# A hybrid decoder trunk on one core: the down projection's B22 loaded twice, and the sums for X3 and X4 moved by one product

## The chip, the cores and the metric

The kernel runs on one core of a Trainium2 chip. The metric is the device time of one execution in microseconds; lower is better. Times of several runs are told as their median. The profile is of one further execution. Engines are called PE (TensorE), PEld (its weight loads), DVE (VectorE), ACT (ScalarE), POOL (GpSimd) and SP (SyncE).

## What is computed

Two layers of a decoder trunk on x of 512 tokens by 1024, all in float32. Each layer is a half-step FFN, a mixer (layer 0 a convolution and a gated unit, layer 1 a multi-scale pool), cross-attention to 256 memory tokens, and a second half-step FFN. So there are four FFNs, and they are where the change lies:

```python
def swiglu_ffn(h, w_gu, w_down):
    gu = h @ w_gu
    gate, up = jnp.split(gu, 2, axis=-1)
    return (jax.nn.silu(gate) * up) @ w_down

f = swiglu_ffn(rms_norm(h, ffn1_pre_g[i]), ffn1_w_gu[i], ffn1_w_down[i])
h = h + 0.5 * rms_norm(f, ffn1_post_g[i])
```

The hidden width is 2816, that is 22 blocks of 128.

## The kernel before

*Precision.* Each float32 operand is split (`split`, L73 to 75) into a rounded part hi, an ACT copy (L74), and the rest lo, a DVE subtraction (L75). A product is three matmuls (`mm3`, L77 to 81: hi by hi, hi by lo, lo by hi). Weights are loaded raw by DMA and split on the chip into `whi` and `wlo`, which have four buffers each (`N_W`); the raw buffers are seven (`N_R`, tag "raw"), each of 512 KB over 128 partitions. Every load of weights in the kernel takes its buffer from these seven.

*An FFN* (`ffn`, L556) goes through the hidden blocks in three parts (`FF_PARTS`): blocks 0 to 7, 8 to 15 and 16 to 21. In each part the gate and up columns are computed in groups of two blocks (`seven`, L292; the very first group by `fm_quad`), and then the part's share of the down projection. For the first two parts the down projection is `seven_tm` (L336): a 2 by 2 block product with seven multiplications where eight are usual. There are four FFNs with two such parts each, eight *down parts* in all. The first of an FFN (`fresh`) writes its results into `f` by ACT copies (L387), the second adds to or subtracts from `f` on DVE (L389, L391).

*A down part.* Weights are the four blocks B11, B12, B21, B22 of 512 rows by 512 columns, each in two raw buffers (two halves of 256 rows, index `kk`). `load` issues plain loads from SP's queue (L347), `put` a second load onto the same buffers that adds to what lies there, from POOL's queue (L352). T1 = B12 + B11 so comes from two loads, T3 = B12 + B22 likewise, and later B21 is added onto T1, which by then is B12 + B11 + B22 (the add of L404, on DVE). X1 to X4 are sums of the activation's quarters: `e` (L394, L400, L417) for X1, X2 and X4, and `r11 -= r21` (L414) for X3; `operand` splits them into buffers of the tag "big". The seven products in order are

| product | bank | weights | operand | result goes to |
|---|---|---|---|---|
| 1 | A | B11 | A11 | f(0,0) |
| 2 | C | T1 | X1 | f(1,1) |
| 3 | A | T1 + B22 | X2 | f(0,1) |
| 4 | B | B21 | A12 | f(0,0) |
| 5 | A | T3 | X3 | f(1,1) |
| 6 | C | B22 | X4 | f(0,1) |
| 7 | A | T1 + B22 + B21 | A22 | f(1,0) |

Each product is 24 matmuls of 512 columns, the first 12 with the first half of the weights (`kk` = 0), and `take` moves or adds its bank's result, one half (`s_`) after the other.

*Order and buffers.* The kernel is written on a layer that gives out tiles' buffers, sets all semaphore waits and puts each engine's instructions in an order of its own: the text sets the precedence, and an instruction may go ahead of earlier ones of its engine that still wait for inputs. Each engine then runs its queue strictly in that order. A raw buffer comes free when the last instruction that reads it has run. In the text before the change, B22's two buffers are loaded once (L358) and read twice: by the adds of L404, and by the split for product 6.

Of the kernel before, what the change touches and what calls it, by code (L numbers as in the profile page):

```python
# [35 lines left out]
def trunk_kernel(tc, x, mem, ffn1_pre_g, ffn1_w_gu, ffn1_w_down, ffn1_post_g,  # L36
# [8 lines left out]
    with ExitStack() as es:  # L45
# [18 lines left out]
        def big(dt=F32R, shape=(P, 4, SEQ)):  # L64
            return sp.tile(list(shape), dt, name="big", tag="big")

        def qt(shape, dt=F32):
            return qp.tile(list(shape), dt, name="q4", tag="q4")
# [4 lines left out]
        def split(hi, lo, src):  # L73
            nc.scalar.copy(out=hi, in_=src)  # L74
            nc.vector.tensor_tensor(out=lo, in0=src, in1=hi.bitcast(F32), op=ALU.subtract)  # L75

        def mm3(ps, lhs, rhs, start, stop, grouped=True):  # L77
            skip = not grouped
            nc.tensor.matmul(out=ps, lhsT=lhs[0], rhs=rhs[0], start=start, stop=skip, skip_group_check=skip)  # L79
            nc.tensor.matmul(out=ps, lhsT=lhs[0], rhs=rhs[1], start=False, stop=skip, skip_group_check=skip)  # L80
            nc.tensor.matmul(out=ps, lhsT=lhs[1], rhs=rhs[0], start=False, stop=stop or skip, skip_group_check=skip)  # L81
# [26 lines left out]
        def ops4():  # L108
            return big(F32R, (P, 2, 4, HALF))
# [124 lines left out]
        def raw_tile(shape):  # L234
            return wp.tile(list(shape), F32, name="raw", tag="raw", bufs=N_R)
# [9 lines left out]
        def parts(raw, shape):  # L245
            hi = wp.tile(list(shape), F32R, name="whi", tag="whi")
            lo = wp.tile(list(shape), F32R, name="wlo", tag="wlo")
            split(hi, lo, raw)
            return hi, lo
# [20 lines left out]
        def psa():  # L270
            return pa.tile([P, 512], F32, name="psa", tag="a")
# [64 lines left out]
        def seven_tm(w, k0, r, a11, f, fresh):  # L336


            def rows(kh, kk, ch):
                u = k0 + 4 * kh + 2 * kk  # L340
                return w[u * P:(u + 2) * P, ch * 512:(ch + 1) * 512].rearrange("(k p) n -> p k n", p=P)

            def load(kh, ch):
                raws = []
                for kk in range(2):
                    raws.append(raw_tile([P, 2, 512]))
                    nc.sync.dma_start(out=raws[kk], in_=rows(kh, kk, ch))  # L347
                return raws

            def put(raws, kh, ch):  # L350
                for kk in range(2):
                    nc.gpsimd.dma_start(out=raws[kk], in_=rows(kh, kk, ch), accum_op=ALU.add)  # L352

            sub, add = ALU.subtract, ALU.add
            t1 = load(0, 1)
            put(t1, 0, 0)
            b11 = load(0, 0)
            b22 = load(1, 1)  # L358
            b21 = load(1, 0)
            r11, r12, r21, r22 = r[0][:, :, :HALF], r[1][:, :, :HALF], r[0][:, :, HALF:], r[1][:, :, HALF:]  # L360

            def operand(src):
                o = ops4()
                split(o[:, 0], o[:, 1], src)
                return o

            banks = {}

            def product(n, raws, ops):
                start = n not in banks  # L370
                if start:
                    banks[n] = [psa(), psa()]
                for kk in range(2):
                    wh = parts(raws[kk], (P, 2, 512))
                    for s_ in range(2):
                        for i in range(2):
                            k = 2 * kk + i
                            cs = slice(s_ * P, (s_ + 1) * P)
                            mm3(banks[n][s_], (ops[:, 0, k, cs], ops[:, 1, k, cs]), (wh[0][:, i], wh[1][:, i]),
                                start and k == 0, k == 3, False)  # L380
                return banks[n]

            def take(th, ch, ps, how):
                for s_ in range(2):
                    dst = f[th][:, s_, ch * 512:(ch + 1) * 512]
                    if how is None:
                        nc.scalar.copy(out=dst, in_=ps[s_])  # L387
                    elif how == "from":
                        nc.vector.tensor_tensor(out=dst, in0=ps[s_], in1=dst, op=sub)  # L389
                    else:  # L390
                        nc.vector.tensor_tensor(out=dst, in0=dst, in1=ps[s_], op=how)  # L391

            e = qt([P, 4, HALF])
            nc.vector.tensor_tensor(out=e, in0=r21, in1=r22, op=sub)  # L394
            x1 = operand(e)
            p1 = product("A", b11, a11)
            if fresh:
                f.append(big(F32, (P, 2, D)))
            take(0, 0, p1, None if fresh else add)
            nc.vector.tensor_tensor(out=e, in0=e, in1=r11, op=sub)  # L400
            x2 = operand(e)
            q5 = product("C", t1, x1)
            for kk in range(2):
                nc.vector.tensor_tensor(out=t1[kk], in0=t1[kk], in1=b22[kk], op=add)  # L404
            if fresh:
                f.append(big(F32, (P, 2, D)))
            take(1, 1, q5, None if fresh else add)
            a12 = operand(r12)
            u2 = product("A", t1, x2)
            t3 = load(0, 1)  # L410
            put(t3, 1, 1)
            put(t1, 1, 0)
            take(0, 1, u2, None if fresh else "from")
            nc.vector.tensor_tensor(out=r11, in0=r11, in1=r21, op=sub)  # L414
            x3 = operand(r11)
            take(0, 0, product("B", b21, a12), add)
            nc.vector.tensor_tensor(out=e, in0=e, in1=r12, op=add)  # L417
            x4 = operand(e)
            take(1, 1, product("A", t3, x3), sub)
            a22 = operand(r22)  # L420
            take(0, 1, product("C", b22, x4), "from")
            take(1, 0, product("A", t1, a22), None if fresh else add)
# [133 lines left out]
        def ffn(pre, w_gu, w_down, post_g, nxt):  # L556
            f = []
            for j0, j1 in FF_PARTS:
# [33 lines left out]
                if ending:  # L592
                    nx = nxt()
                    last_weights(w_down, j0, n, wk, False)
                    tm_last(hid, wk, n, post_g, nx, f)
                else:
                    seven_tm(w_down, j0, r, a11, f, not f)
# [442 lines left out]
```

## Time and profile before

| | us |
|---|---|
| median of 3 runs | 2033.12 |
| the runs | 2029.88, 2033.5, 2033.12 |
| the profiled execution | 2035.78 |
| its span, first to last instruction | 2034.1 |
| PE busy | 1962.7 |
| DVE busy | 1488.5 |
| ACT busy | 1037.4 |
| POOL busy | 234.0 |

A busy time is the sum over an engine's instructions, overlaps counted once. "Granted clock" is the share of the full 2.4 GHz that PE was given; at 0.5 it runs at 1.2 GHz. Times in a timeline are us from the start of the span. In a timeline a row is: start, duration, engine, line, operation, written tile and read tiles, shapes, count; in square brackets stands how long the engine had been idle and what ended that. The down parts' first L404 lies at 103.2, 227.6, 833.4, 957.8, 1183.3, 1308.2, 1763.7 and 1888.3 us; "the first part" below is the one at 103, "the second part" that at 227.

### The profile page before, as it was taken

How to read it: one execution, taken by the hardware profiler on the slowest of the kernel's cores; microseconds unless marked ns; L12 is line 12 of the kernel's file. 1: busy time of each engine (PE TensorE's matmuls, PEld its weight loads, DVE VectorE, ACT ScalarE, POOL GpSimd, SP SyncE). 2: the span in 40 equal slices, each digit the busy share in tenths (PEclk: the TensorE clock that was granted, in tenths of full speed). 3: DMA queues.
4: the chain of work that ended last, by engine and by line, in shares of the span. 5: the costliest groups of instructions: out<-in, count | busy, mean ns of one | idle time of the engine just before them, and what ended most of it. 6: DMA issues, size and time to landing. Idle time of an engine off the chain costs nothing. (4 is left out here: it accounts for less than half of the span.)

```text
span 2034.1 us, 31756 instructions
## 1 busy us (share of the span) xinstructions
PE 1962.7 (96%) x12841; PEld 1788.2 (88%) x12841; DVE 1488.5 (73%) x1831; ACT 1037.4 (51%) x1477; POOL 234.0 (12%) x229
## 2 busy tenths in 40 slices
PE   7999999998999999999999999999999999999998
PEld 7979889888878879899898979989878879989797
DVE  6776877799956558777886877787666648776875
ACT  6555445543555355555454555445535545545452
POOL 1111110122011011110101111110000001111100
PEclk9999999999999999999999999999999999999999
DMA  6877685323642145787873668696152225787771
GB/s 198 217 166 198 161 212 155 110 89 124 225 148 94 52 114 139 172 202 181 191 214 73 169 156 204 169 215 197 53 186 73 83 52 145 184 200 198 172 189 44
DMA packets 245929, 311.51 MB, mean 153 GB/s; under 512 B 9500, under 2 KB 189300, under 8 KB 244758
## 3 DMA queue, kind: packets, MB, share of 16 engines
q1 hardware_dynamic: 189158, 233.93, 35.9%
q0 software_dynamic: 56448, 75.51, 21.9%
q8 instruction: 100, 1.64, 0.3%
q14 instruction: 47, 0.39, 0.1%
q10 hardware_dynamic: 176, 0.05, 0.0%
HBM read 303.15 MB, written 6.29 MB: 152 GB/s over the span
## 5 line engine op out<-in xcount | busy, mean ns | idle before, releaser
L79 PE MATMUL psa<-big,whi 128*128 128x256 f32 (+1 forms) x3056 | 885.2, 291 | 6.2 <-ACT big L74 4.5
L81 PE MATMUL psa<-big,wlo 128*128 128x256 f32 (+1 forms) x3056 | 885.4, 290 | 5.6 <-DVE wlo L75 5.6
L80 PE MATMUL psa<-big,whi 128*128 128x256 f32 (+1 forms) x3056 | 887.1, 291 | 0.8 <-DVE big L75 0.8
L74 ACT CAST whi<-raw 128x1024 fp32r<-128x1024 f32 x522 | 544.3, 1049 | 622.8 <-PE psa L80 275.4
L75 DVE TENSOR_TENSOR wlo<-raw,whi 128x1024 fp32r<-128x1024 f32 x522 | 635.6, 1225 | 283.1 <-ACT whi L74 280.6
L79 PEld LDWEIGHTS psa<-big,whi 128*128 128x128 f32 x3056 | 587.6, 193 | 16.7 <-ACT big L74 8.3
L81 PEld LDWEIGHTS psa<-big,wlo 128*128 128x128 f32 x3056 | 588.0, 193 | 13.6 <-DVE wlo L75 6.7
L80 PEld LDWEIGHTS psa<-big,whi 128*128 128x128 f32 x3056 | 588.7, 193 | 9.1 <-DVE big L75 1.8
L79 PE MATMUL psa<-whi,big 128*128 128x512 f32 x864 | 341.5, 397 | 19.2 <-ACT whi L74 11.5
L80 PE MATMUL psa<-wlo,big 128*128 128x512 f32 x864 | 340.4, 394 | 6.1 <-DVE wlo L75 6.1
L81 PE MATMUL psa<-whi,big 128*128 128x512 f32 x864 | 339.3, 395 | 0.5
L79 PEld LDWEIGHTS psa<-whi,big 128*128 128x128 f32 x864 | 162.9, 189 | 60.7 <-ACT whi L74 16.6
L80 PEld LDWEIGHTS psa<-wlo,big 128*128 128x128 f32 x864 | 164.0, 190 | 42.7 <-DVE wlo L75 9.7
L81 PEld LDWEIGHTS psa<-whi,big 128*128 128x128 f32 x864 | 163.8, 190 | 39.7 <-DVE big L75 5.8
L302 POOL DMA_DIRECT2D raw<-in_ffn_w_gu_dram x40 | 51.6, 1289 | 611.9 <-DMA raw<-in_ffn_w_gu_dram 419.2
L158 POOL TENSOR_TENSOR r<-m,nhalf 128x1 f32<-128x1 f32 x74 | 49.0, 662 | 461.0 <-DVE m L532 182.3
L352 POOL DMA_DIRECT2D raw<-in_ffn_w_down_dram x48 | 57.3, 1193 | 332.7 <-DMA raw<-in_ffn_w_down_dram 229.5
L729 DVE SCALAR_TENSOR_TENSOR big<-big,par 128x511 f32<-128x511 f32 (+29 forms) x120 | 85.7, 767 | 0.0
L79 PE MATMUL psa<-big 128*128 128x512 f32 (+1 forms) x224 | 80.9, 363 | 0.8 <-ACT big L74 0.8
L297 POOL DMA_DIRECT2D raw<-in_ffn_w_gu_dram x40 | 53.0, 1326 | 244.7 <-DMA raw<-in_ffn_w_gu_dram 223.4
L80 PE MATMUL psa<-big 128*128 128x512 f32 (+1 forms) x224 | 80.7, 360 | 0.0
L81 PE MATMUL psa<-big 128*128 128x512 f32 (+1 forms) x224 | 80.2, 359 | 0.0
(150 smaller groups left out, 1658.2 us busy)
## 6 DMA issues: line engine op xcount, KB each, us to landing
raw<-in_ffn_w_gu_dram SPq DMA_DIRECT2D x216, 512.0 KB, 4.8
raw<-in_ffn_w_down_dram SPq DMA_DIRECT2D x104, 512.0 KB, 4.0
raw<-in_ffn_w_gu_dram POOLq DMA_DIRECT2D x80, 512.0 KB, 7.8
raw<-in_ffn_w_down_dram POOLq DMA_DIRECT2D x48, 512.0 KB, 6.1
raw<-in_xa_w_kv_dram SPq DMA_DIRECT2D x32, 512.0 KB, 3.5
raw<-in_ev_w_in_dram SPq DMA_DIRECT2D x16, 512.0 KB, 4.3
raw<-in_xa_w_q_dram SPq DMA_DIRECT2D x16, 512.0 KB, 3.7
raw<-in_xa_w_o_dram SPq DMA_DIRECT2D x16, 512.0 KB, 3.9
```

Of the source, the lines that this page charges most:

```text
L74: nc.scalar.copy(out=hi, in_=src)
L75: nc.vector.tensor_tensor(out=lo, in0=src, in1=hi.bitcast(F32), op=ALU.subtract)
L79: nc.tensor.matmul(out=ps, lhsT=lhs[0], rhs=rhs[0], start=start, stop=skip, skip_group_check=skip)
L80: nc.tensor.matmul(out=ps, lhsT=lhs[0], rhs=rhs[1], start=False, stop=skip, skip_group_check=skip)
L81: nc.tensor.matmul(out=ps, lhsT=lhs[1], rhs=rhs[0], start=False, stop=stop or skip, skip_group_check=skip)
L158: nc.gpsimd.tensor_tensor(out=r, in0=m, in1=nhalf.broadcast_to([P, n]), op=ALU.pow)
L297: nc.gpsimd.dma_start(out=t1, in_=fm_rows(w, 0, ca), accum_op=ALU.add)
L302: nc.gpsimd.dma_start(out=t3, in_=fm_rows(w, 1, cb), accum_op=ALU.add)
L352: nc.gpsimd.dma_start(out=raws[kk], in_=rows(kh, kk, ch), accum_op=ALU.add)
L729: nc.vector.scalar_tensor_tensor(out=acc[:, c, s_:], in0=z[:, c, :SEQ - s_], scalar=par[:, c, CONV - 1 - s_:CONV - s_], in1=acc[:, c, s_:] ...
```

## The change

B22 is loaded a second time, after T3's loads and the second load onto T1; product 6 reads this second load, and the first load is read by the adds of L404 alone. The raw buffers of the first load can then be given to a load that is asked for later, and the next one in the text is T3's. The sum for X3 (L414) and its split now stand in the text behind product 4 and its takes, and the sum for X4 (L417) and its split behind product 5 and its takes; in the text before, each stood ahead of that product. The products, their order and the takes are the same.

```diff
             t3 = load(0, 1)
             put(t3, 1, 1)
             put(t1, 1, 0)
+            b22 = load(1, 1)
             take(0, 1, u2, None if fresh else "from")
+            take(0, 0, product("B", b21, a12), add)
             nc.vector.tensor_tensor(out=r11, in0=r11, in1=r21, op=sub)
             x3 = operand(r11)
-            take(0, 0, product("B", b21, a12), add)
+            take(1, 1, product("A", t3, x3), sub)
             nc.vector.tensor_tensor(out=e, in0=e, in1=r12, op=add)
             x4 = operand(e)
-            take(1, 1, product("A", t3, x3), sub)
             a22 = operand(r22)
             take(0, 1, product("C", b22, x4), "from")
             take(1, 0, product("A", t1, a22), None if fresh else add)
```

## Rows read from the trace of the kernel before

**Rows 1.** The page's first part: busy time, share of span, instructions.
```profile
PE 1962.7 (96%) x12841; PEld 1788.2 (88%) x12841; DVE 1488.5 (73%) x1831; ACT 1037.4 (51%) x1477; POOL 234.0 (12%) x229
```

**Rows 2.** Windows, PE alone: length, busy (matmuls), granted clock, DMA share, GB/s.
```profile
127.70:142.70 15.00, 11.75 (x49) 1.00 0.74 177
252.10:267.10 15.00, 13.37 (x51) 0.89 0.97 236
858.00:873.00 15.00, 11.67 (x50) 1.00 0.72 172
982.30:997.30 15.00, 13.30 (x50) 0.89 0.96 234
1207.80:1222.80 15.00, 12.72 (x47) 0.89 0.69 153
1332.70:1347.70 15.00, 13.36 (x58) 1.00 1.02 255
1788.20:1803.20 15.00, 12.97 (x48) 0.89 0.71 168
1912.80:1927.80 15.00, 13.22 (x57) 1.00 1.00 254
1524.00:1539.00 15.00, 15.00 (x68) 1.00 0.30 95
```

**Rows 3.** Timeline of ACT: T3's hi (first part), X3's hi (second part).
```profile
130.87 1.04 ACT L74 CAST whi<-raw 128x1024 fp32r<-128x1024 f32 x1 [6.43 <-DMA raw<-in_ffn_w_down_dram]
...
247.56 1.05 ACT L74 CAST big<-big 128x1024 fp32r<-128x1024 f32 x1 [1.71 <-PE psa L81]
```

**Rows 4.** Timeline of DVE in the first part.
```profile
104.84 1.23 DVE L404 TENSOR_TENSOR raw<-raw 128x1024 f32<-128x1024 f32 x1
...
131.94 1.23 DVE L75 TENSOR_TENSOR wlo<-raw,whi 128x1024 fp32r<-128x1024 f32 x1 [6.25 <-ACT whi L74]
```

**Rows 5.** Waits of SP's queue, first and second part: total us, times, longest.
```profile
SPq L347 <- DVE wlo L75: 18.7, 2, 16.3
...
SPq L347 <- DVE wlo L75: 22.4, 2, 20.0
```

**Rows 6.** Timeline of POOL in the first part.
```profile
111.63 1.20 POOL L352 DMA_DIRECT2D raw<-in_ffn_w_down_dram  x1 [3.62 <-DVE wlo L75]
...
122.73 1.20 POOL L352 DMA_DIRECT2D raw<-in_ffn_w_down_dram  x1 [6.31 <-DMA raw<-in_ffn_w_down_dram]
```

**Rows 7.** Timeline of DVE in the second part.
```profile
229.16 1.23 DVE L404 TENSOR_TENSOR raw<-raw 128x1024 f32<-128x1024 f32 x1
...
244.04 1.22 DVE L414 TENSOR_TENSOR big<-big 128x1024 f32<-128x1024 f32 x1
...
249.78 1.22 DVE L417 TENSOR_TENSOR q<-q,big 128x1024 f32<-128x1024 f32 x1
...
252.95 0.69 DVE L391 TENSOR_TENSOR big<-big,psa 128x512 f32<-128x512 f32 x1 [0.22 <-PE psa L81]
```

**Rows 8.** All 80 plain loads of L347: time from issue to landing.
```profile
DMA to landing us min/median/max: 3.2/3.9/5.6
```

**Rows 9.** All 48 accumulating loads of L352: time from issue to landing.
```profile
DMA to landing us min/median/max: 5.5/6.1/9.6
```

**Rows 10.** DMA queues from 100 to 150 us: packets, MB, share of 16 engines.
```profile
q1 hardware_dynamic: 4489, 5.20, 33.0%
```

**Rows 11.** Windows, second part: PE, PEld, DVE, ACT, POOL busy, clock, DMA share, GB/s.
```profile
228.00:248.00 20.00, 19.16 (x88) 15.10 (x88) 19.77 (x20) 10.10 (x11) 3.58 (x3) 1.00 0.53 100
248.00:268.00 20.00, 18.37 (x73) 14.39 (x72) 16.82 (x19) 9.06 (x10) 3.42 (x3) 0.91 0.91 238
```

**Rows 12.** The same view, in the gate/up group after the first part.
```profile
148.00:168.00 20.00, 20.00 (x166) 19.88 (x165) 13.24 (x14) 9.97 (x13) 3.14 (x3) 1.00 0.99 222
```

**Rows 13.** The one L352 issued between 238.0 and 239.5 us: time to landing.
```profile
DMA to landing us min/median/max: 5.7/5.7/5.7
```

## The prediction

> **What bounds the kernel now.** I read the page's busy times first. TensorE (PE) is busy 1962.7 of 2034.1 us, DVE 73%, ACT 51% [rows 1]: a PE kernel, so an edit off PE pays only where PE stands still or runs slowly. Busy time hides the second kind (a matmul at half clock counts as busy), so the next view counts matmuls in equal windows. In a stretch without a stall, 15 us hold 68 matmuls of 512 columns. In the eight down parts the 15 us that cover products A (T3, X3) and C (B22, X4) hold 49, 51, 50, 50, 47, 58, 48 and 57 [rows 2]: 410 where 544 would fit, 134 missing. At 15/68 us each, 134 are 29.6 us, 1.5% of the span. 17.2 us of it (78 matmuls) is in the first part of each FFN, whose takes are ACT copies (here "fresh"), 12.4 us (56) in the second. Some of it is clock: in four windows the granted clock is 0.89, so 11% of their 15 us is lost to the lower level (1.2 GHz), after PE had waited in them; in the other four it stays at 1.00 [rows 2].
>
> Who is waited for: in the first part ACT idles 6.43 us for a w_down DMA and starts that buffer's hi copy at 130.87 [rows 3]; DVE, idle for 6.25 us, does its lo at 131.94 [rows 4]; only then can PE go on. The buffer is T3's second half. SP had waited 16.3 us (20.0 us in the second part) before it could issue the plain load, held by a DVE weight split [rows 5]: all seven raw buffers were in use (T1 2, B22 2, B21 2, T3's first half 1), and the next to come free was B21's, split for product B. POOL issued its accumulating load only when the plain one had landed, at 122.73 [rows 6], and that landed 8 us later, at ACT's 130.87.
>
> **The change, part by part.** *T3 early.* B22's first load is no longer read by product C, so its buffers come free at the two adds of L404. The first add ends at 106.07 in the first part [rows 4] and at 230.39 in the second [rows 7]. T3's second half takes that buffer: SP can issue it there, where its waits of 16.3 and 20.0 us [rows 5] ended at about 118.4 and 246.5. A plain load lands in 3.2 to 5.6 us, an accumulating one in 5.5 to 9.6 [rows 8, 9]. With both at their worst and 1 us of POOL, T3 is there at 106.1 + 5.6 + 9.6 + 1 = 122.3, some 8.5 us ahead of today's 130.87, and a fresh part loses only 17.2/4 = 4.3 us. In the second part it is there at 246.6, while PE comes to T3's second half 12 matmuls after 252.9 (where B ends, [rows 7]), at 255.6. So the wait for this DMA goes in all eight parts: up to 29.6 us.
>
> *B22 again.* 2 loads of 512 KB in each of 8 parts, 16 in all. SP's queue moved 5.20 MB in 33.0% of 50 us [rows 10], so 0.524 MB is 1.7 us of all 16 DMA engines, 3.3 us for a part. In the second part the DMA share is 0.53 and then 0.91 over 20 us each [rows 11], 28.8 us of 40; with 3.3 more, in 36.5 us, it is 0.88. Bounds: nothing, or 3.3 x 8 = 27 us if DMA became the bound. I take nothing, because the nearest row is the stretch behind the first part: share 0.99 with PE busy 20.00 of 20 [rows 12]. The first new load gets B22's second old buffer (some 3 us after T3's), the second the B21 buffer that T3's second half has today, at about 246.5. It lands by 252.1; product C starts at 252.9 + 24 x 0.22 = 258.2. Behind it on SP stand the next gate/up loads; today they stand behind T3's load, which waits for the same buffer, so they don't start later. That wait of 20.0 us is the cover; without it each load would cost its issue on SP, under 0.5 us.
>
> *POOL.* T3's second accumulating load moves ahead of T1's two. If POOL waits for T3's plain load (106.1 + 5.6 = 111.7 at worst; T1's first goes at 111.63 today, [rows 6]), T1's come about 1.3 us later, for the last product, over 20 us after. Nothing.
>
> *The sums.* L414 and L417 keep their length (1.22 us each) and move in the text. DVE's queue isn't in text order: L417 stands in the text behind product B's takes and yet ran at 249.78, ahead of the L391 at 252.95 [rows 7]. So an instruction goes in when its inputs are there and nothing ahead of it in the text is ready. Ahead of L414 I expect at most two weight splits and two takes, 1.22 and 0.69 us by the lengths of [rows 7]: 244.04 + 3.8 = 247.9. X3's hi copy starts at 247.56 today [rows 3], so X3 would have its hi at 250.2 and its lo at 251.5; product A (T3, X3) starts at 252.9. No stall, with 1.4 us to spare: bounds 0 and, with L414 behind L391, rival 3. I take 0, by L417's place. In fresh parts DVE has more room (6.25 us idle, [rows 4]).
>
> *What is late next.* DVE. In the second part it is busy 19.77 of 20 and then 16.82 of 20 us [rows 11], 3.41 idle in 40, and the stall to be removed there is 17 matmuls, 3.75 us. It can't all go: DVE would have to work without a gap, while it waits at product ends (0.22 us, [rows 7]). Bounds of what stays: 0 (its last splits belong to the next gate/up group, where DVE is busy 13.24 of 20 us, [rows 12]) to 1.8 us in each such part; I take 0.9, in the middle, 3.6 us for four. For fresh parts 0 to 0.8 each; I take 0.3, 1.2 us, nearer to nothing because of the 6.25 us idle.
>
> **Sum.** 29.6 - 3.6 - 1.2 = 24.8 us. Against the profiled execution's own 2035.78 us: 2011.0. That execution lies 2.7 us above the median of the runs (2033.12; 2029.88 to 2033.5), so for the median 2008.3; I say 2008. Its own range: 2002 (29.6 gone, and runs' spread) to 2014 (the high bounds, 10.4, stay).
>
> **A rule against it.** T3's second accumulating load now goes where DVE is saturated, and it is issued by POOL. The rows speak against a conflict: the one of T1's issued at 238.5, while DVE was busy 19.77 of 20 us [rows 11], landed in 5.7 us [rows 13], near the shortest of all 48, 5.5 [rows 9]. The Trainium skill, "SBUF — State Buffer", § SBUF: two separate sides, warns that a DMA issued from POOL stands still while DVE holds the port that both share, since POOL can't write its descriptors; the page limits that to DVE's 2-port modes. Read broadly it gives rival 2; the trace agrees with the limit.
>
> **Rivals.**
> 1. *DVE takes the stall's place in the second parts.* There nothing is gained, in fresh parts 17.2 - 1.2 = 16.0: 2033.1 - 16.0 = 2017. For it: 19.77 of 20 [rows 11]. Against: over 3 us idle in the 20 that follow. It decides if DVE needs more than the 36.3 us that would be left of the 40. Chance 0.12.
> 2. *T3's early load is starved until DVE pauses* in the second parts, at about 252.7 [rows 7], so lands as late as now: 2017 again. Chance 0.02.
> 3. *The sums stand behind B's takes (slower).* If DVE's queue has L414 after L391, it starts at 252.95 + 0.69 = 253.6, X3's hi is there at 255.9 (1.22 and 1.05 us), its lo at 257.1: product A waits 3.0 us and then some 1.2 more, and the clock falls as in the 0.89 windows, 0.11 x 15 = 1.7 us. 5.9 for the 3.7 removed (29.6/8), +2.2 x 8: 2033 + 18 = 2051. It costs from an L414 start after 250.6 on (252.9 less 1.22 and 1.05). For it: the text now puts it there. Against: L417 [rows 7]. Chance 0.09.
> 4. *The freed buffers don't go to T3* but to another load that asks first; T3's second half waits for B21's as now: 2033. Against: T3's is the oldest load that waits. Chance 0.07.
>
> **How the numbers follow.** Forecast 0.70, with its own time, 2008. The range goes to 2021, over rivals 1 and 2 with the runs' spread of 4 us, and down to 2001 (29.6 gone and a run on the low side of that spread); 3 and 4 are left out, 0.16. A measurement of this kernel tells about 0.2%, 4 us. Faster 0.70 + 0.12 + 0.02 = 0.84, same 0.07, slower 0.09.
>
> **What will show it.** Right: T3's second plain load on SP at the end of L404's first add; 64 to 68 matmuls in windows like those of [rows 2], without 0.89; ACT no longer idle for a w_down DMA. Wrong: L414 behind L391 (rival 3); an SP wait of 16 to 20 us for T3 (rival 4); DVE without a gap and PE waiting for lo parts in second parts (rival 1); plain loads landing well after 5.6 us, which would make DMA the bound after all.

## The result, and the profile after

| | before | after |
|---|---|---|
| median of 4 runs, us | 2033.31 | 2006.44 |
| lowest to highest | 2029.88 to 2037.34 | 2001.77 to 2007.58 |
| the profiled execution | 2035.78 | 2006.68 |
| its span | 2034.1 | 2005.0 |
| PE busy | 1962.7 | 1951.0 |
| DVE busy | 1488.5 | 1488.6 |

The ratio after to before is 0.9863, with a 95% interval of 0.9839 to 0.9887: 1.4% faster, 26.9 us by the medians and 29.1 us between the two profiled spans. In the code after, the sums are L416 (X3) and L419 (X4).

The windows over PE at the same place of each down part as in [rows 2] (length, busy with matmuls, granted clock, DMA share, GB/s), kernel after:

```profile
126.90:141.90 15.00, 15.00 (x68) 1.00 0.93 232
247.00:262.00 15.00, 15.00 (x68) 1.00 0.88 236
848.60:863.60 15.00, 15.00 (x68) 1.00 0.93 232
968.80:983.80 15.00, 15.00 (x68) 1.00 0.85 222
1190.60:1205.60 15.00, 15.00 (x68) 1.00 0.95 231
1310.80:1325.80 15.00, 15.00 (x68) 1.00 0.85 225
1765.90:1780.90 15.00, 15.00 (x68) 1.00 0.94 230
1886.00:1901.00 15.00, 15.00 (x68) 1.00 0.86 222
```

All 134 missing matmuls are back, 544 of 544, and the clock is full in all eight. Whole down parts say the same. From the start of the first of its 168 matmuls to the start of the last, a part took 41.8 to 44.0 us before; after, a first part of an FFN takes 39.3 us and a second part 39.6. Over the eight that is 29.7 us less, so the gain lies inside the down parts.

PE's own busy time fell by only 11.7 us of the 29.1. Some 6.6 us of this were matmuls at the lower clock (0.11 of 15 us in four windows), and the rest was mostly PE's slow start behind a wait, where a matmul is recorded with 0.50 us or more and not 0.39. Both count as busy. That is why the windows, and not the busy share, showed the size of the stall.

SP's timeline, kernel after, around the end of L404's first add of the first part (start us, us, engine, line), and then the longest waits of SP's L347 in the second part (total us, times, longest):

```profile
105.25 0.37 SPq L347 DMA_DIRECT2D raw<-in_ffn_w_down_dram  x1
...
SPq L347 <- DVE wlo L75: 13.9, 2, 11.5
SPq L347 <- DVE raw L404: 6.6, 2, 4.0
```

The releaser of a load is now L404, the add that reads B22's first load; the add starts at 104.00 and takes 1.23 us, and the load is issued at 105.25. The wait of 11.5 us that remains for the split of B21's buffer is that of the reload of B22, for product 6; the waits of 16.3 and 20.0 us of [rows 5] had been T3's, for product 5.

DVE's timeline in the second part, kernel after (start, duration, engine, line, operation, tiles, shapes, count, idle before):

```profile
241.91 1.22 DVE L416 TENSOR_TENSOR big<-big 128x1024 f32<-128x1024 f32 x1
...
244.78 1.22 DVE L75 TENSOR_TENSOR big<-big 128x1024 fp32r<-128x1024 f32 x1
...
247.05 0.68 DVE L391 TENSOR_TENSOR big<-big,psa 128x512 f32<-128x512 f32 x1
247.95 0.69 DVE L391 TENSOR_TENSOR big<-big,psa 128x512 f32<-128x512 f32 x1 [0.23 <-PE psa L81]
248.56 1.22 DVE L419 TENSOR_TENSOR q<-q,big 128x1024 f32<-128x1024 f32 x1
```

L416 stands in the text behind the L391s and runs 5.1 us ahead of the first of them; X3's lo is ready at 246.0. L419, which ran ahead of the L391 in [rows 7], now runs behind both, and nobody waits for it.

### The profile page after: what moved, and what is told of

It is laid out like the page before. It is cut to its first block, busy times and chain, and to the rows that moved or that the text cites. A ratio compares the mean times of both kernels' runs of the same rounds, so it can differ in the third digit from the quotient of the medians.

```text
span 2005.0 us, 31807 instructions
## 1 busy us (share of the span) xinstructions
PE 1951.0 (97%) x12841; PEld 1784.3 (89%) x12841; DVE 1488.6 (74%) x1831; ACT 1038.3 (52%) x1477; POOL 233.8 (12%) x229
## 4 chain that ended last, share of the span: by engine, by line
PE 80%; DVE 8%; issue 5%; ACT 3%; POOL 2%; DMA 1%; POOLq 0%; ACTq 0%; SPq 0%; DVEq 0%
PE psa L81 26%; PE psa L80 26%; PE psa L79 26%; DVE wlo L75 2%; POOL r L158 1%; DVE big L75 1%; DVE big L730 1%; ACT q L175 1%; ACT whi L74 1%; PE tps L182 1%; DMA raw<-in_ffn_w_gu_dram 1%; ACT q L166 1%; DVE h L479 0%; DVE raw L404 0%; DVE q L394 0%
## 5 line engine op out<-in xcount | busy, mean ns | idle before, releaser
L81 PEld LDWEIGHTS psa<-whi,big 128*128 128x128 f32 x864 | 162.2, 188 | 39.3 <-DVE big L75 5.8
L352 POOL DMA_DIRECT2D raw<-in_ffn_w_down_dram x48 | 57.4, 1227 | 261.9 <-DMA raw<-in_ffn_w_down_dram 187.0
```

## The experiments

A word on names: "reload" is B22's second load, "the move" the later place of the two sums. The theory: T3's second half was late because its plain load had no buffer, and anything that gives it one early wins some 25 to 30 us; the move is worth nothing.

### The reload alone

The kernel before with one line more:

```diff
             put(t1, 1, 0)
+            b22 = load(1, 1)
             take(0, 1, u2, None if fresh else "from")
```

> B22 is loaded a second time as in the changed kernel, but the sums for X3 and X4 stay where they were in the text. Theory (the gain is T3's early buffer, and the sums' place is worth nothing): 2003 to 2011 us, T3's second plain load on SP some 3 us after the part's first L404 begins, 24 matmuls of 0.227 us in products 5 and 6 without a gap in all eight parts. Rival (the sums had to move, because DVE is without a gap in second parts): X3's sum keeps its place ahead of B21's splits, so a lo part comes late there and each second part loses 0.5 to 1.5 us more: 2009 to 2013 us, with PE waiting for DVE in second parts and not in fresh ones.

Measured: 2005.77 us (2004.96 to 2010.95), ratio 0.9853 (0.9829 to 0.9877). Two of its windows, of a first and a second part:

```profile
127.10:142.10 15.00, 15.00 (x68) 1.00 0.97 235
...
1313.40:1328.40 15.00, 15.00 (x67) 1.00 0.88 241
```

The whole gain is there without the move: this kernel and the changed one can't be told apart.

### The move alone

The changed kernel without that line.

```diff
             put(t1, 1, 0)
-            b22 = load(1, 1)
             take(0, 1, u2, None if fresh else "from")
```

> The sums for X3 and X4 are moved as in the changed kernel, B22 is loaded once. Theory (buffer): 2029 to 2037 us, SP still waits 16 to 20 us for T3's second buffer, and the 15 us windows still hold about 50 matmuls. Rival (a good part of the gain comes from DVE's new order): 2010 to 2025 us.

Windows over PE at the same place as in [rows 2], four of the eight:

```profile
125.20:140.20 15.00, 11.38 (x48) 1.00 0.72 172
249.90:264.90 15.00, 12.09 (x40) 0.77 0.73 168
...
983.80:998.80 15.00, 11.31 (x38) 0.77 0.70 153
...
1337.10:1352.10 15.00, 11.77 (x44) 0.89 0.75 169
```

Measured: 2045.96 us (2040.32 to 2048.43, 8 runs), ratio 1.0051 (1.0036 to 1.0066). Both expectations failed: it is neither like before nor partly better, but 12 us slower by the medians (7 to 13 by the interval). The eight windows hold 361 matmuls where before held 410: 49 fewer, at 15/68 us 10.8 us, and the second parts carry nearly all of it (40, 38, 44 and 44, where [rows 2] has 51, 50, 58 and 57). In the second part POOL issues T3's last accumulating load at 247.04, and ACT waits for it until 254.82; the timelines of POOL and ACT of this kernel:

```profile
247.04 1.20 POOL L352 DMA_DIRECT2D raw<-in_ffn_w_down_dram  x1 [7.47 <-DVE big L389]
...
254.82 1.04 ACT L74 CAST whi<-raw 128x1024 fp32r<-128x1024 f32 x1 [7.70 <-DMA raw<-in_ffn_w_down_dram]
```

Issue to landing of that one load, first in this kernel, then of the same load in the kernel before:

```profile
DMA to landing us min/median/max: 7.8/7.8/7.8
...
DMA to landing us min/median/max: 5.6/5.6/5.6
```

The line of POOL names L389 as the releaser, but the plain load under it had landed only at 246.5, some 0.5 us before; in both kernels POOL follows that landing by 0.5 us. With X3's sum out of the way DVE does B21's split sooner, so T3's loads go out sooner too: the accumulating one 21.7 us after the part's first L404, where it was 22.8 (both counted, like the times of the first L404s given before, from where DVE starts to wait for that add; in the kernel before the add itself starts at 229.16 and not at 227.6). The next gate/up load on SP moves further: it goes out 0.7 us behind T3's, where it was 1.9 us behind (252.20 against 250.30). T3's load then takes 2.2 us longer, so it lands 1.1 us later in the part than it did.

It is so in all four second parts: 7.7 to 7.8 us against 5.5 to 5.7, with SP's next load 0 to 0.8 us behind against 1.8 to 1.9. PE's longest wait there is 2.3 to 3.2 us, where it was 1.4 to 1.6, and the clock falls in all four second parts (0.77, 0.77, 0.89 and 0.89), where it fell in two [rows 2].

That the neighbouring loads are what slows T3's is read from the order of the times; no run isolated it. The Trainium skill, "DMA: Bandwidth & Descriptors", § Issuing engines are not separate DMA queues, says that loads issued from different engines interleave on the same 16 DMA engines. By that, a POOL load can be slowed by SP's loads beside it; the trace fits this (7.8 against 5.6 us), but doesn't show it.

### T3 in a buffer of another pool, nothing else

The kernel before, with T3's second half in a spare activation buffer instead of a raw one: B22 is loaded once, and no sum moves.

```diff
-            def load(kh, ch):
+            def load(kh, ch, spare=False):
                 raws = []
                 for kk in range(2):
-                    raws.append(raw_tile([P, 2, 512]))
+                    raws.append(qt([P, 2, 512]) if spare and kk else raw_tile([P, 2, 512]))
...
-            t3 = load(0, 1)
+            t3 = load(0, 1, True)
```

> The kernel before, in which T3's second half lies in a buffer of the tag q4 instead of one of the seven raw buffers; B22 is loaded once, no sum is moved. Theory (what counts is that T3's second half has a buffer early, wherever it comes from): 2002 to 2011 us, as the changed kernel; if the 16 extra loads cost anything, by that much faster than it, at most 3 us. Rival (the second load of B22 matters by itself): slower than the changed kernel by over 4 us. Rival (the q4 buffers are held by the gate/up groups until late): T3's load goes out late, 2025 to 2033 us.

Measured: 2005.65 us (2004.92 to 2008.73), ratio 0.9857 (0.9836 to 0.9878). SP's timeline of the first part, and the windows of the first two parts:

```profile
101.17 0.42 SPq L347 DMA_DIRECT2D q<-in_ffn_w_down_dram  x1
...
126.80:141.80 15.00, 15.00 (x68) 1.00 0.87 199
246.90:261.90 15.00, 15.00 (x67) 1.00 0.80 206
```

So the second load of B22 does nothing by itself: it is a way to end the life of B22's buffers early. Its price is also bounded. This kernel reaches the same time with 16 loads fewer, so 16 loads of 512 KB cost nothing that can be measured here; the interval of a ratio is some 5 us to either side.

### The sums held behind product B's takes

Rival 3 of the prediction, made to happen: in the changed kernel L416 is held in its place in the text.

```diff
             take(0, 0, product("B", b21, a12), add)
-            nc.vector.tensor_tensor(out=r11, in0=r11, in1=r21, op=sub)
+            tc.keep_in_program_order(nc.vector.tensor_tensor(out=r11, in0=r11, in1=r21, op=sub))
             x3 = operand(r11)
```

> The changed kernel, with X3's sum held behind product 4's takes in DVE's queue in all eight parts (rival 3 of the prediction made true). Price of that rival: product 5 waits 3.0 us for X3's hi and some 1.2 for its lo, and where the clock falls 1.7 more; over eight parts 34 to 47 us above the changed kernel's 2006: 2040 to 2053 us. Other view (X3 has slack and DVE's other work comes forward into the gap): 2015 to 2030 us. If the sum's place were of no weight: 2006.

Measured: 2045.61 us (2041.86 to 2048.49, 7 runs), ratio 1.0053 (1.0036 to 1.0071). DVE in the second part, the longest wait of PE's list (total, times, longest), then two of the eight windows, all of which stand at 0.89:

```profile
250.89 1.28 DVE L391 TENSOR_TENSOR big<-big,psa 128x512 f32<-128x512 f32 x2
252.08 1.22 DVE L416 TENSOR_TENSOR big<-big 128x1024 f32<-128x1024 f32 x1
...
PE psa L79 <- ACT big L74: 36.5, 22, 3.1
...
125.30:140.30 15.00, 11.91 (x46) 0.89 0.81 174
250.40:265.40 15.00, 11.87 (x45) 0.89 0.72 177
```

In the kernel after, that wait is 11.6 us in 14 cases; so there are 8 more of 3.1 us, one in each part. Rival 3 had said 3.0 us, and 2051 in all. All told it costs 39.2/8 = 4.9 us a part, which is about the wait and the 1.7 us of the clock; the further wait of 1.2 us for X3's lo, which made it 5.9, did not come. So the gain hangs also on L416's place in DVE's queue: behind the takes, the changed kernel would have been slower than before.

### More work for DVE in the second parts

The changed kernel; in the four second parts A22's lo split is done three times more, some 3.4 us of DVE a part.

```diff
             a22 = operand(r22)
+            for _ in range(0 if fresh else 3):
+                nc.vector.tensor_tensor(out=a22[:, 1], in0=r22, in1=a22[:, 0].bitcast(F32), op=sub)
             take(0, 1, product("C", b22, x4), "from")
```

> The changed kernel with A22's lo split done four times in place of once in the four second parts: 3 more DVE instructions of 1.14 us from start to start, 3.4 us for a part, 13.7 us in all, the same values written again. It asks what DVE's lack of gaps in second parts is worth (rival 1 of the prediction). If DVE sets the time there: 2006 + 10 to 14 = 2016 to 2020 us, PE waiting for lo parts in product 7 or in the gate/up group behind. If the splits behind them belong to the next group and its room takes them up: 2005 to 2011 us.

Measured: 2011.6 us (2011.27 to 2011.95), ratio 0.988 (0.9859 to 0.9901): 5.2 us above the changed kernel, 1.3 us a part of the 3.4 added. That lies between the two expectations, just above the second. One of PE's waits in this kernel (total us, times, longest):

```profile
PE psa L81 <- DVE big L423: 3.7, 4, 0.9
```

This wait, once in each second part and not there in the kernel after, is product 7 waiting for the added splits. So about 2 us of DVE's time (3.4 less 1.3) was free there, though the windows of the changed kernel look full. The run puts the work ahead of product 7 alone; how much room products 5 and 6 have, it doesn't tell. The windows are, PE, PEld, DVE, ACT, POOL busy, clock, DMA share and GB/s, second part, kernel after:

```profile
222.50:242.50 20.00, 19.18 (x89) 15.19 (x88) 19.74 (x21) 9.65 (x10) 4.77 (x4) 1.00 0.90 195
242.50:262.50 20.00, 20.00 (x90) 16.52 (x89) 19.74 (x21) 10.23 (x10) 3.85 (x3) 1.00 0.85 229
```

DVE is busy 39.48 of 40 us, and in the second window PE is busy throughout: part of DVE's work belongs to the next gate/up group and is done ahead of need. Its sum at 261.25, for one, is L321, a line of that group, whose first matmul behind the part comes at some 264.

### More DMA

The changed kernel with four copies of 512 KB more in every down part, from HBM to HBM, issued on SP right behind B22's reload. The edit, without the lines that set up `spare` and `last_load`:

```diff
             b22 = load(1, 1)
+            with tc.issue_after(last_load[0].ins):
+                for n_, d_ in enumerate(spare):
+                    nc.sync.dma_start(out=d_, in_=w[(k0 + 2 * n_) * P:(k0 + 2 * n_ + 2) * P, 0:512])
```

> The changed kernel with four plain copies of 512 KB from the down weights to spare space in HBM in each down part, behind the second load of B22 on SP's queue: 2 MB more for a part, where the change itself added 1 MB. By 1.7 us of all DMA engines for each it would take the DMA work of a second part from 35 of 40 us to some 42. Theory (DMA has room and the part's loads are early enough): 2005 to 2011 us, with longer landings but PE without new waits in the parts. Rival (DMA is the next bound right behind the change): the gate/up loads behind them come late, 2 to 6 us for each part, 2020 us or more.

Measured: 2005.95 us (2002.17 to 2007.72), ratio 0.9849 (0.9821 to 0.9877): no change from the changed kernel. Its window in the second part, and the copies' line (count, KB each, us to landing):

```profile
242.00:262.00 20.00, 20.00 (x90) 16.56 (x89) 19.43 (x21) 10.24 (x10) 2.56 (x2) 1.00 1.06 322
...
spare<-in_ffn_w_down_dram SPq DMA_DIRECT2D x32, 512.0 KB, 7.6
```

The DMA share goes from 0.85 to 1.06 in that stretch, and PE is busy for all of its 20 us. With 2 MB more a part, DMA still isn't the bound of the down parts.

### Product B moved to second place

In the kernel after, PE waits once in a down part: at the start of product 2, for the hi of X1, which ACT makes after DVE's sum. PE's timeline, first and second part:

```profile
110.48 0.50 PE L79 MATMUL psa<-whi,big 128*128 128x512 f32 x1 [0.77 <-ACT big L74]
...
230.62 0.50 PE L79 MATMUL psa<-whi,big 128*128 128x512 f32 x1 [0.77 <-ACT big L74]
```

Product B (B21, A12) needs no sum; put second, it covers the sum for X1. Its split of B21 then also runs two products earlier, so that B21's buffers come free early as well. Two kernels: the changed one with B second, and the kernel *before* with B second and B22 loaded once.

```diff
             e = qt([P, 4, HALF])
-            nc.vector.tensor_tensor(out=e, in0=r21, in1=r22, op=sub)
-            x1 = operand(e)
+            a12 = operand(r12)
             p1 = product("A", b11, a11)
...
             take(0, 0, p1, None if fresh else add)
+            nc.vector.tensor_tensor(out=e, in0=r21, in1=r22, op=sub)
+            x1 = operand(e)
+            take(0, 0, product("B", b21, a12), add)
...
-            a12 = operand(r12)
...
-            take(0, 0, product("B", b21, a12), add)
```

> The changed kernel with product B (B21, A12) moved from fourth to second place in the down part, ahead of X1's product; A12 is split first, X1 after it. What it asks: each part still has PE waiting 0.93 us, and some 0.4 us of slow starts, for X1, which needs the last quarter of the activation. Theory (A12 is ready earlier than X1, so product 2 starts on time and X1 has 5.4 us more): 1.3 us less in each of eight parts, 2006 less 10: 1994 to 1999 us. Rival (no buffer of the tag big is free for A12 so early, or X2 then comes late): the wait moves behind product 2 or 3, 2003 to 2010 us.

> The kernel before with product B moved to second place, B22 loaded once and the sums in their old place. With B second, B21's first buffer is split for it and comes free before the first L404, so T3's second half can have it early without a second load of B22. Theory: both waits go, T3's (29 us over the kernel) and X1's (10 us): 1994 to 1999 us, within 3 us of the run that keeps the second load. Rival (T3's second half gets its buffer only after a later split): 2015 to 2033 us.

Measured: with the reload 1998.3 us (1996.99 to 1998.94), ratio 0.9814 (0.9793 to 0.9835); without it 1998.88 us (1996.18 to 2000.23), ratio 0.9816 (0.9794 to 0.9839). Both came as expected and beat the changed kernel by some 8 us. The second kernel, 40 us of the first and of the second part, SP's longest wait of the first part, and then the same stretches of the kernel after:

```profile
102.60:142.60 40.00, 40.00 (x185) 33.26 (x184) 36.68 (x35) 25.36 (x29) 8.64 (x7) 1.00 0.90 197
221.50:261.50 40.00, 39.52 (x178) 32.24 (x177) 39.03 (x41) 20.66 (x21) 8.62 (x7) 1.00 0.81 181
...
SPq L347 <- DVE wlo L75: 7.6, 3, 2.8
```

```profile
104.00:144.00 40.00, 39.17 (x175) 31.87 (x174) 36.05 (x35) 24.86 (x29) 8.65 (x7) 1.00 0.92 215
224.20:264.20 40.00, 39.18 (x172) 31.44 (x170) 39.04 (x41) 20.94 (x21) 8.62 (x7) 1.00 0.89 209
```

SP's wait of 16.3 us is down to 2.8 with each block loaded once. PE's 0.83 us of waiting goes in the first part; 0.48 of 0.82 stays in the second, at later products. Four times 0.83 and four times 0.34 are 4.7 us of waiting. The rest of the gain lies in the same parts. These are the first and the last matmul of the fourth FFN's first part, in the kernel after and then in this one:

```profile
1743.08 0.40 PE L79 MATMUL psa<-whi,big 128*128 128x512 f32 x1
...
1782.36 0.39 PE L81 MATMUL psa<-whi,big 128*128 128x512 f32 x1
...
1736.04 0.40 PE L79 MATMUL psa<-whi,big 128*128 128x512 f32 x1
...
1774.03 0.39 PE L81 MATMUL psa<-whi,big 128*128 128x512 f32 x1
```

A first part so goes from 39.3 to 38.0 us, and the second parts go from 39.6 to 38.9: 8.1 us over the eight, against 7.6 between the medians. The wait of 0.77 us for X1 cost a first part 1.3 us, with the slow start behind it.

## Why the prediction was right

It said 2008 us, 2001 to 2021; the median is 2006.44. Step by step:

- **The stall, 29.6 us.** Right in size: 134 missing matmuls all came back, the down parts got 29.7 us shorter and the span 29.1 us. The difference between these two lies outside the parts, within the spread of single runs. The price of one matmul is rough: in the timelines they start 0.227 us apart, and 15/68 is less since a window counts those cut by its ends too; at 0.227, 134 are 30.4 us.
- **T3 early.** Right: issued at the end of L404's first add (105.25 and 225.39), so the waits of 16.3 and 20.0 us are gone. The reload alone (2005.77) and the other buffer (2005.65) show that this is the whole cause.
- **What stays because of DVE, 3.6 + 1.2 us.** The mis-sized term of the sum: nothing stays. All eight windows hold 68, those of the second parts too. The prediction counted DVE's 3.41 idle us against a stall of 3.75 us and took the middle between all and nothing of DVE's work being needed in those 40 us. Nothing was the right end: DVE works 39.48 of 40 us, and products 3 to 7 don't wait for it. By the run with more DVE work about 2 us of room is left at product 7, so rival 1 was that far off there. Without the term the sum is 29.6, against 29.1 measured.
- **From the sum to 2008.** In part luck. The prediction kept 4.8 us that weren't kept, and it took off 2.7 us because the profiled execution before lay that far above its median; the profiled execution after lies only 0.24 us above its own. The two errors go opposite ways. With 29.6 and the 2.7 us alone it would have said 2003.5.
- **The reload's cost, nothing.** Right, over a range of 0 to 27 us. Loads did become slower: the plain loads' median went from 3.9 to 4.2 us, the longest from 5.6 to 6.8; the accumulating ones' median from 6.1 to 7.8 (longest 9.3, within the 9.6 of [rows 9]). The sign "plain loads landing well after 5.6 us" so showed in part, without DMA becoming the bound. The margin of over 8 us at T3 took that up, and even four further copies cost nothing. All landings of after, plain loads and then accumulating ones:

```profile
DMA to landing us min/median/max: 3.2/4.2/6.8
...
DMA to landing us min/median/max: 5.7/7.8/9.3
```

- **POOL.** Right: T3's second accumulating load goes ahead of T1's two, at 110.06; T1's first follows at once (the same row) and T1's other one at 114.38. Rival 2 didn't come: in the second part that load goes out at 230.33 and lands in 5.8 us, while DVE is busy 13.74 us of the 14 from 222.5 on, and ACT's wait for it is gone in second parts as in first ones.

```profile
110.06 2.42 POOL L352 DMA_DIRECT2D raw<-in_ffn_w_down_dram  x2 [4.06 <-DMA raw<-in_ffn_w_down_dram]
114.38 1.20 POOL L352 DMA_DIRECT2D raw<-in_ffn_w_down_dram  x1 [1.90 <-DVE wlo L75]
```

- **The sums, nothing.** Right in the place and the price, in this kernel: L416 runs ahead of the takes with X3's lo ready at 246.0, some 1.7 us ahead of product 5, which starts at about 247.7 (1.4 us were worked out). Its margin is small, and the held-back version shows what hangs on it: -27 us turns to +12. What the prediction didn't see is that the move is not harmless by itself. Without the reload it makes the kernel 12 us slower: it reorders DVE's splits, which release raw buffers, which release loads, and T3's load then takes longer, for a reason that no run isolated. With the reload T3 is out of that chain, and the move costs nothing.
- **Rival 4**, the freed buffer going to another load, didn't come: L347's release by L404 shows it.

## What to carry to other kernels

When a load waits for a buffer, look for the last reader of the buffer that it will get, and see whether that reader can be given its own copy or moved earlier: reading B22 twice from one buffer cost 29 us of 2034, and loading it again cost nothing. Better still is an order of work in which the last reader comes early, as with product B in second place, which gains more and loads nothing twice. And an engine that is 99% busy isn't the bound by that alone; add some work to it in a run and see what comes of it.

## What the runs showed of the hardware

- A wait of PE costs more than its length, and not the same each time. In the second parts of the kernel before PE stands 1.6 to 1.8 us for T3's hi, in two pieces. In two of the four the granted clock then fell, to 0.89 over the window, and the part took 43.4 us; in the other two it stayed at 1.00, and the part took 41.8 and 41.9 us, against 39.6 without the wait. After waits of 3.1 us in one piece it was 0.89 in 8 of 8 parts. What decides between the two outcomes after the shorter waits, no run shows. Product 5's matmuls in the held-back run start 0.43 us apart at the lower clock (1.2 GHz); in the kernel after they start 0.23 us apart at 2.4 GHz:

```profile
255.57 0.63 PE L79 MATMUL psa<-whi,big 128*128 128x512 f32 x1
255.99 0.63 PE L80 MATMUL psa<-wlo,big 128*128 128x512 f32 x1
...
247.98 0.39 PE L80 MATMUL psa<-wlo,big 128*128 128x512 f32 x1
248.21 0.39 PE L81 MATMUL psa<-whi,big 128*128 128x512 f32 x1
```

- The same accumulating load of 512 KB landed in 5.5 to 5.7 us in one kernel and in 7.7 to 7.8 us in another that differs in the order of work alone, in four of four parts.
- The DMA share stood at 1.06 over 20 us, with 322 GB/s, while PE was busy in all 20 us. A share above 1 also says that the figure isn't an exact share.
